# Token sums of the feed-forward weights begun while the output projection still runs

## The chip, the cores and the metric

One core of a Trainium2 chip runs one program. The time is the device time of one execution in microseconds; a kernel's time is the median of several executions. Its engines are TensorE (PE, matmuls, with weight loads as PEld), VectorE (DVE), ScalarE (ACT), GpSimd (POOL) and SyncE (SP). SP, ACT and POOL also issue DMA transfers, which 16 DMA engines carry out. Each engine works through its own list of instructions in order, and waits on semaphores for what others produce. The order of each list is made when the program is built, by a scheduler that simulates the program.

## The reference

Two layers on a sequence of 1024 tokens of width 1024, batch 1, in float32. Layer 0 mixes tokens by windowed attention, layer 1 by a gated linear recurrence in both directions; each has cross attention heads beside it. What matters here is the seam between a layer's mixer and its feed-forward part:

```
h = h + rmsnorm(concat(o, cross) @ w_out, g1)        # output projection
u = rmsnorm(h, g2)
gate, up = split(u @ w_in)                           # 1024 -> 2 x 2816
f = (gelu(depthwise_conv3(gate) + b) * up) @ w_out2  # 2816 -> 1024
h = h + rmsnorm(f, g3)
```

## The kernel before

Every float32 product is made of three products of operands split into a high and a low part (wh and wl for weights, uh and ul for tokens): high by high, high by low, low by high. ScalarE makes the high part by a cast, VectorE the low part by a subtraction.

The **output projection** (class WOut, method finish) works on row tiles of 128 tokens, eight of them, in two column halves of 512. The first half makes y0 for all eight rows (one tile of 128 x 8 x 512) and POOL multiplies it with the gain g1. The second half then goes row by row, n = 0 to 7: TensorE makes 12 x 3 matmuls from oh and ol (split from `or`, which SP loads); VectorE multiplies with g1 (y1); the row's mean square goes to POOL, which raises it to the power -1/2 (prs); VectorE adds y0 and y1, scaled by prs, to the old row x (L537, two instructions); the row is stored (h1d); norm_T normalizes it: the sum of squares on ScalarE, the power on POOL (nrs), the scaling on VectorE (nu, L124), eight 128 x 128 transposes on TensorE (pt, L132), and the split into uh and ul. For n = 4 to 7 the differences dw (POOL, then VectorE) and xd (VectorE) are made too.

The **first feed-forward stage** (function ffn) multiplies 1024 x 1024 tokens with 22 weight pieces f of 1024 x (2 x 128). It replaces eight block products by seven, with sums of weight blocks and sums of token blocks. Per f the weights are four tiles: st holds blocks as they are, sx and sy hold sums. sx is loaded twice with the same 256 KB block by SP (L638), then POOL issues a DMA that adds 512 KB from memory to it (L641). sy is loaded by SP (512 KB, L639), then POOL issues two DMAs: one adds half of sx to half of sy (L642), the next half of sy to the other half (L643); each waits for the one before. They are called the token sums' weights, or the sums. Products 1 and 2 use st and write the banks X and Y; product 5 (sx) and 3 (sy) write V; product 6 (sy, with u6h and u6l), 7 (sx, with u7h and u7l) and 4 (st, with u4h and u4l) write X. The functions load, weights, operand and prod make these.

The first two f, and products 1 and 2 of the third, are written out in first_units: while the projection's last rows are still on their way, TensorE already runs products 1 and 2 on the tokens that are done; products 5, 6, 3, 7 and 4 follow. From then on the f follow in a steady loop.

Memory sets when the sums can begin. The tiles sx and sy belong to the pool of the FFN (fp), two of each. They are placed where the projection's tiles were, so SP's loads into them and POOL's adds wait for whatever used that place last. The order of POOL's and SP's instructions is the scheduler's; `tc.high_priority` puts a part ahead in it, and `behind(...)` makes an instruction issue after another.

## Time and profile before

| | us |
|---|---|
| median of 3 runs | 2749.36 |
| lowest and highest | 2745.89, 2750.08 |
| profiled execution, its own time | 2745.05 |
| its span in the trace | 2743.3 |
| TensorE busy in it | 2665.1 (97%) |

The mean clock that TensorE was granted is 0.992 of full speed. Layer 0's projection, second half, is at about 530 to 600 us of the trace and its first feed-forward products start at about 596; in layer 1 they start at about 2088. Row tile n = 6 has its transposes at 595.27 and 2087.36, row tile n = 7 at 607.10 and 2099.19. TensorE's matmuls overlap: a matmul is listed with about 0.39 us, but with nothing to wait for the next one starts 0.227 us later. A number in brackets behind a row is the time the engine stood idle before it, with what ended that wait.

### The profile page before, as it was taken

What the parts mean: (1) busy time and instruction counts of PE and PEld (TensorE: products, weight loads), DVE (VectorE), ACT (ScalarE), POOL (GpSimd) and SP (SyncE); (2) the same over time, 40 slices, a digit from 0 to 9 for tenths busy, and PEclk for the clock granted to TensorE, in tenths of its full rate; (3) what the DMA queues carried; (4) which work ended last, traced back from release to release, by engine and by line L of the source; (5) the groups of instructions that cost most, each with busy time, mean ns of one, the idle gap of its engine ahead of it and who ended that gap; (6) DMA issues with size and microseconds to landing.
All of it is one profiled execution on the core that took longest, in us unless ns stands there. A gap on an engine that the chain in (4) does not pass through costs nothing.

```text
span 2743.3 us, 37508 instructions
## 1 busy us (share of the span) xinstructions
PE 2665.1 (97%) x13448; PEld 2225.2 (81%) x13448; DVE 1818.9 (66%) x3039; ACT 1398.6 (51%) x2558; POOL 489.5 (18%) x537
## 2 busy tenths in 40 slices
PE   8999999999999999999999999999998999999998
PEld 7888887787888888887888888888787888887887
DVE  6588777677565555477686777868567756556446
ACT  6367667544444445454454545545454544444443
POOL 1231120221111100031232231312122111110012
PEclk9999998999999999999999999999999999999999
DMA  7683213668777757673234541111467777774666
GB/s 281 207 177 83 66 45 101 195 184 201 201 195 196 198 148 242 197 261 126 73 135 110 118 93 55 43 58 34 142 211 189 189 201 203 199 197 151 228 192 230
DMA packets 217035, 435.79 MB, mean 159 GB/s; under 512 B 20752, under 2 KB 77456, under 8 KB 211216
## 3 DMA queue, kind: packets, MB, share of 16 engines
q1 hardware_dynamic: 188416, 334.55, 37.5%
q0 software_dynamic: 25408, 92.29, 16.5%
q10 hardware_dynamic: 3024, 6.55, 0.6%
q8 instruction: 106, 1.74, 0.3%
q14 instruction: 81, 0.66, 0.1%
HBM read 338.42 MB, written 117.96 MB: 166 GB/s over the span
## 4 chain that ended last, share of the span: by engine, by line
PE 87%; DVE 6%; DMA 3%; ACT 2%; issue 2%; POOL 1%; SPq 0%; DVEq 0%; POOLq 0%; ACTq 0%
PE X L564 29%; PE V L564 10%; PE pj L84 8%; PE pj L85 7%; PE pj L86 7%; PE Y L564 4%; PE pb L84 3%; PE pb L85 3%; PE pb L86 3%; PE po L1192 1%; PE pa L1144 1%; PE pt L361 1%; PE pa L1124 1%; PE pu L1168 1%; DMA sx<-in_ffw_dram 1%
## 5 line engine op out<-in xcount | busy, mean ns | idle before, releaser
L89 DVE TENSOR_TENSOR wl<-st,wh 128x1024 fp32r<-128x1024 f32 (+1 forms) x242 | 262.9, 1090 | 351.7 <-ACT wh L89 332.0
L89 ACT CAST wh<-st 128x1024 fp32r<-128x1024 f32 (+1 forms) x242 | 225.6, 934 | 293.0 <-PE X L564 190.4
L84 PE MATMUL pj<-uh,wh 128*128 128x512 f32 x512 | 206.4, 403 | 6.4 <-DVE xl L89 4.6
L564 PE MATMUL X<-wl,wh 128*128 128x512 f32 x528 | 204.9, 390 | 0.3 <-DVE wl L89 0.3
L564 PE MATMUL X<-wh,wl 128*128 128x512 f32 x528 | 204.9, 390 | 0.0
L85 PE MATMUL pj<-ul,wh 128*128 128x512 f32 x512 | 203.2, 397 | 0.0
L86 PE MATMUL pj<-uh,wl 128*128 128x512 f32 x512 | 203.0, 396 | 0.0
L564 PE MATMUL X<-wh 128*128 128x512 f32 x528 | 199.8, 390 | 1.4 <-DVE c L920 1.4
L84 PE MATMUL pj<-wh,uh 128*128 128x384 f32 (+1 forms) x512 | 190.8, 373 | 0.4 <-DVE v L303 0.4
L85 PE MATMUL pj<-wl,uh 128*128 128x384 f32 (+1 forms) x512 | 186.9, 365 | 0.0
L86 PE MATMUL pj<-wh,ul 128*128 128x384 f32 (+1 forms) x512 | 186.7, 365 | 0.0
L564 PE MATMUL V<-uh,wl 128*128 128x512 f32 x352 | 137.2, 390 | 1.1 <-DVE wl L89 1.1
L564 PE MATMUL V<-uh,wh 128*128 128x512 f32 x352 | 137.8, 391 | 0.0
L564 PE MATMUL V<-ul,wh 128*128 128x512 f32 x352 | 137.7, 391 | 0.0
L80 DVE TENSOR_TENSOR wl<-st,wh 128x1024 fp32r<-128x1024 f32 (+1 forms) x86 | 107.4, 1255 | 26.2 <-ACT wh L79 25.3
L79 ACT CAST wh<-st 128x1024 fp32r<-128x1024 f32 (+1 forms) x96 | 96.7, 1014 | 51.1 <-PE pj L85 31.6
L1138 POOL TENSOR_TENSOR E<-EP,q 128x256 f32<-128x256 f32 x64 | 53.2, 831 | 371.0 <-DVE EP L1131 270.6
L84 PEld LDWEIGHTS pj<-uh,wh 128*128 128x128 f32 x512 | 97.2, 190 | 26.8 <-DVE xl L89 5.5
L564 PEld LDWEIGHTS X<-wh 128*128 128x128 f32 x528 | 99.1, 188 | 22.5 <-issue 1.8
L564 PEld LDWEIGHTS X<-wl,wh 128*128 128x128 f32 x528 | 99.1, 188 | 21.3 <-DVE wl L89 0.7
L564 PEld LDWEIGHTS X<-wh,wl 128*128 128x128 f32 x528 | 99.1, 188 | 20.7
L86 PEld LDWEIGHTS pj<-uh,wl 128*128 128x128 f32 x512 | 97.2, 190 | 19.6
(324 smaller groups left out, 7335.4 us busy)
## 6 DMA issues: line engine op xcount, KB each, us to landing
st<-hid SPq DMA_DIRECT2D x154, 256.0 KB, 3.2
st<-in_ffw_dram SPq DMA_DIRECT2D x110, 256.0 KB, 3.2
w2s<-in_ffw_dram POOLq DMA_DIRECT2D x24, 1024.0 KB, 7.8
st<-in_ffw_dram SPq DMA_DIRECT2D x44, 512.0 KB, 3.7
sx<-in_ffw_dram SPq DMA_DIRECT2D x88, 256.0 KB, 4.1
sy<-in_ffw_dram SPq DMA_DIRECT2D x44, 512.0 KB, 5.6
sx<-in_ffw_dram POOLq DMA_DIRECT2D x44, 512.0 KB, 8.3
hid<-tt SPq DMA_DIRECT2D x88, 256.0 KB, 4.4
```

Of the source, the lines that this page charges most:

```text
L79: act.copy(h[:, :n], raw)
L80: (eng or dve).tensor_tensor(l[:, :n], raw, h[:, :n].bitcast(F32), op=ALU.subtract)
L84: pe.matmul(o, ah, bh, start=first, stop=False)
L85: pe.matmul(o, ah, bl, start=False, stop=False)
L86: pe.matmul(o, al, bh, start=False, stop=last)
L89: return act.copy(h, src), dve.tensor_tensor(l, src, h.bitcast(F32), op=ALU.subtract)
L361: pe.transpose(tp[:, j, :], sm[:, j, c * P:(c + 1) * P], ident)
L564: pe.matmul(o, x, y, start=new, stop=e, skip_group_check=not first)
L1124: pe.matmul(pa[:, c, :], E2[:, cs], E1[:, cs], start=True, stop=True)
L1138: pool.tensor_tensor(gl, pl_, ql, op=ALU.mult)
L1144: pe.matmul(pa[eo:eo + n, c, lo:lo + n], G[:, c * P + eo:c * P + eo + n], G[:, c * P + lo:c * P + lo + n], start=True, stop=True, tile_pos ...
L1168: r["marks"][1:] = [pe.matmul(pu[:, c, :], kT[:, c, :], r["v"][:, 4 * b + c, :], start=True, stop=True)]
```

## The change

y0 is no longer one tile of the projection's pool but four tiles of two rows each, with the tags sx, sx, sy, sy, in a new pool `ys` that lives until the first feed-forward stage has ended. The FFN's sx and sy come from that pool too. So the place of y0's rows 0 and 1 becomes the first sx, that of rows 2 and 3 the second sx, that of rows 4 and 5 the first sy, that of rows 6 and 7 the second sy, each as soon as its two rows have been added to x.

The sums of f = 0 and 1 are written into the loop of the projection's second half: behind row n = 1 the two loads of the first sx, behind n = 2 its add, behind n = 3 and 4 the same for the second sx, behind n = 5 the load of the first sy, behind n = 6 its two adds, behind n = 7 the load of the second sy. The two adds of the second sy are in first_units. The loads of f = 2 and 3 are no longer issued behind a mark, and the conv constants (cw, cb, ncw) have a pool of their own, allocated later. The second feed-forward stage and the steady loop keep their code.

```diff
+    def sums_x(l, f, pl):
+
+        sx = pl.tile([P, 1024], F32, tag="sx", bufs=2, name="sx")
+        for c in range(2):
+            nc.sync.dma_start(sx[:, c * 512:(c + 1) * 512], A["ffw1"][l, f, :, :512])
+        return sx
+
+    def add_x(l, f, sx):
+        pool.dma_start(sx, A["ffw1"][l, f, :, 512:1536], accum_op=ALU.add, max_dma_last_dim=8192)
+
+    def sums_y(l, f, pl):
+        sy = pl.tile([P, 1024], F32, tag="sy", bufs=2, name="sy")
+        nc.sync.dma_start(sy, A["ffw1"][l, f, :, 1024:])
+        return sy
+
+    def add_y(sx, sy):
+        pool.dma_start(sy[:, :512], sx[:, :512], accum_op=ALU.add, max_dma_last_dim=8192)
+        pool.dma_start(sy[:, 512:], sy[:, :512], accum_op=ALU.add, max_dma_last_dim=8192)
...
+            self.yq = tc.alloc_tile_pool(name=f"ys{l}", bufs=1, side="right", reuse_waits="tile")
+            y2 = [self.yq.tile([P, 2, 512], F32, tag=t, bufs=2, name="y0") for t in ("sx", "sx", "sy", "sy")]
+            y0 = {t: y2[n // 2][:, n % 2, :] for n, t in enumerate(self.order)}
...
-            y0 = wp.tile([P, NT, 512], F32, bufs=1, name="y0")
...
+                if n in (1, 3):
+                    self.sx.append(sums_x(l, n // 2, self.yq))
+                elif n in (2, 4):
+                    add_x(l, n // 4, self.sx[-1])
+                elif n in (5, 7):
+                    self.sy.append(sums_y(l, n // 6, self.yq))
+                elif n == 6:
+                    add_y(self.sx[0], self.sy[0])
...
-        def load(f, a1=None, a22=None):
+        def load(f, a1=None):
...
-            if a22 is None:
-                a22 = raw()[:, :512]
-            sx, sy = [fp.tile([P, 1024], F32, tag=t, bufs=2, name=t) for t in ("sx", "sy")]
-            for c in range(2):
-                nc.sync.dma_start(sx[:, c * 512:(c + 1) * 512], w[:, :512])
-            last_load[0] = nc.sync.dma_start(sy, w[:, 1024:])
+            a22 = raw()[:, :512]
+            sx, sy = sums_x(l, f, wo.yq), sums_y(l, f, wo.yq)
             nc.sync.dma_start(a22, w[:, 512:1024])
-            pool.dma_start(sx, w[:, 512:1536], accum_op=ALU.add, max_dma_last_dim=8192)
-            pool.dma_start(sy[:, :512], sx[:, :512], accum_op=ALU.add, max_dma_last_dim=8192)
-            pool.dma_start(sy[:, 512:], sy[:, :512], accum_op=ALU.add, max_dma_last_dim=8192)
+            add_x(l, f, sx)
+            add_y(sx, sy)
...
-                raws = {f: load(f, a1[f], a22[:, f * 512:(f + 1) * 512]) for f in range(2)}
+                r = raw()
+                a22 = [r[:, f * 512:(f + 1) * 512] for f in range(2)]
+                for f in range(2):
+                    nc.sync.dma_start(a22[f], A["ffw1"][l, f, :, 512:1024])
+                raws = {f: (a1[f], wo.sx[f], wo.sy[f], a22[f]) for f in range(2)}
                 a1.append(raw(A["ffw1"][l, 2, :, 1024:]))
+                add_y(wo.sx[1], wo.sy[1])
...
-            with behind(last_load):
-                raws[2] = load(2, a1[2])
-                raws[3] = load(3)
+            raws[2] = load(2, a1[2])
+            raws[3] = load(3)
```

The scheduler then orders the engines anew. POOL, layer 0, from the nrs of row n = 5 to the end of the projection, before (sx_6595 and sy_6596 are f = 0, sx_6604 and sy_6605 f = 1; dw_6439 and dw_6535 belong to rows 6 and 7):

```order
L102 TENSOR_TENSOR nrs_6340<-nms_6338,nhalf_76 128x1
L128 TENSOR_TENSOR dw_6439<-uh_78,ul_79 128x512
L102 TENSOR_TENSOR prs_6426<-pms_6424,nhalf_76 128x1
L102 TENSOR_TENSOR nrs_6436<-nms_6434,nhalf_76 128x1
L128 TENSOR_TENSOR dw_6535<-uh_78,ul_79 128x512
L102 TENSOR_TENSOR prs_6522<-pms_6520,nhalf_76 128x1
L102 TENSOR_TENSOR nrs_6532<-nms_6530,nhalf_76 128x1
L641 DMA sx_6595<-in_ffw1_dram 128x1024
L641 DMA sx_6604<-in_ffw1_dram 128x1024
L642 DMA sy_6596<-sx_6595 128x512
L642 DMA sy_6605<-sx_6604 128x512
```

The same stretch now (sx_5991 and sy_6375 are f = 0, sx_6179 and sy_6571 f = 1):

```order
L102 TENSOR_TENSOR nrs_6354<-nms_6352,nhalf_76 128x1
L410 DMA sy_6375<-sx_5991 128x512
L128 TENSOR_TENSOR dw_6455<-uh_78,ul_79 128x512
L411 DMA sy_6375<-sy_6375 128x512
L102 TENSOR_TENSOR prs_6442<-pms_6440,nhalf_76 128x1
L102 TENSOR_TENSOR nrs_6452<-nms_6450,nhalf_76 128x1
L128 TENSOR_TENSOR dw_6553<-uh_78,ul_79 128x512
L102 TENSOR_TENSOR prs_6540<-pms_6538,nhalf_76 128x1
L410 DMA sy_6571<-sx_6179 128x512
L102 TENSOR_TENSOR nrs_6550<-nms_6548,nhalf_76 128x1
L411 DMA sy_6571<-sy_6571 128x512
```

Both adds of f = 0's sy now stand ahead of row 6's prs, and the first add of f = 1's sy ahead of row 7's nrs; the two adds of sx stand further ahead, behind the nrs of rows 1 and 3. In layer 1 the first two come directly one behind the other, ahead of dw.

VectorE, layer 0, from the last nu on, before:

```order
L124 SCALAR_TENSOR_TENSOR nu_6528<-x_6512,nrs_6532,g2_5755 128x1024
L89 TENSOR_TENSOR wl_6633<-st_6613,wh_6632 128x1024
L135 TENSOR_TENSOR dw_6535<-dw_6535,pt_6537 128x512
L89 TENSOR_TENSOR ul_79<-pt_6545,uh_78 128x4x128
L140 TENSOR_TENSOR xd_5487<-pt_6545,dw_6535 128x4x128
L89 TENSOR_TENSOR ul_79<-dw_6535,uh_78 128x4x128
L720 TENSOR_TENSOR u_6620<-Y_6618,s1_6660 128x512
L720 TENSOR_TENSOR u_6621<-Y_6619,s1_6687 128x512
L579 TENSOR_SCALAR ncw_6569<-cw_6565 128x66
L89 TENSOR_TENSOR wl_6718<-sx_6595,wh_6717 128x1024
L89 TENSOR_TENSOR wl_6722<-sx_6604,wh_6721 128x1024
L591 SCALAR_TENSOR_TENSOR u6l_6586<-xd_5487,u6h_6585 128x1024 x2
```

And now:

```order
L124 SCALAR_TENSOR_TENSOR nu_6546<-x_6530,nrs_6550,g2_5761 128x1024
L89 TENSOR_TENSOR wl_6640<-st_6618,wh_6639 128x1024
L89 TENSOR_TENSOR wl_6725<-sx_5991,wh_6724 128x1024
L89 TENSOR_TENSOR wl_6729<-sx_6179,wh_6728 128x1024
L748 TENSOR_TENSOR u_6628<-Y_6626,s1_6694 128x512
L135 TENSOR_TENSOR dw_6553<-dw_6553,pt_6555 128x512
L89 TENSOR_TENSOR wl_6737<-sy_6375,wh_6736 128x1024
L89 TENSOR_TENSOR ul_79<-pt_6563,uh_78 128x4x128
L140 TENSOR_TENSOR xd_5487<-pt_6563,dw_6553 128x4x128
L89 TENSOR_TENSOR ul_79<-dw_6553,uh_78 128x4x128
L622 SCALAR_TENSOR_TENSOR u6l_6598<-xd_5487,u6h_6597 128x1024 x2
L89 TENSOR_TENSOR wl_6741<-sy_6571,wh_6740 128x1024
```

The low parts of both sx and of the first sy now stand ahead of row 7's last ul, the one of `ul<-dw`, which product 5 needs; the first u stands ahead of nu, and ncw further behind.

More of the change, by code (lines that the diff above doesn't have):

```diff
@@ L510, in finish @@
                 if t in self.part:
-                    dve.tensor_tensor(y0[:, t, :], ps, self.part[t], op=ALU.add)
+                    dve.tensor_tensor(y0[t], ps, self.part[t], op=ALU.add)
                 else:
-                    act.copy(y0[:, t, :], ps)
-                sumsq(wp, y0[:, t, :], s0[:, t:t + 1])
+                    act.copy(y0[t], ps)
+                sumsq(wp, y0[t], s0[:, t:t + 1])
             with tc.issue_after(after.ins):
@@ L522, in finish @@
             for t in self.order:
-                pool.tensor_tensor(y0[:, t, :], y0[:, t, :], g1[:, :512], op=ALU.mult)
+                pool.tensor_tensor(y0[t], y0[t], g1[:, :512], op=ALU.mult)
             for n, t in enumerate(self.order):
@@ L535, in finish @@
                 rs = rstd_of(wp, ss, 1, D, "p")
-                for c, y in ((slice(0, 512), y0[:, t, :]), (slice(512, 1024), y1)):
+                for c, y in ((slice(0, 512), y0[t]), (slice(512, 1024), y1)):
                     dve.scalar_tensor_tensor(x[:, c], y, rs[:, 0:1], x[:, c], op0=ALU.mult, op1=ALU.add)
@@ L587, in ffn @@
             B[k] = tuple(u2p.tile([P, 4, 512], F32R, name=f"u{k}{c}") for c in "hl")
+        cp = tc.alloc_tile_pool(name=f"cw{l}", bufs=1, reuse_waits="tile")
+        cw = cp.tile([P, NF, 3], F32, name="cw")
+        cb = cp.tile([P, NF], F32, name="cb")
+        nc.sync.dma_start(cw, A["conv_w"][l])
+        nc.sync.dma_start(cb, A["conv_b"][l])
+        ncw = cp.tile([P, NF, 3], F32, name="ncw")
+        dve.tensor_scalar_mul(ncw, cw, -1.0)
         def nsplit(h, l_, src):
```

14 lines of the change are left out of this document (4 added, 10 removed).

## The prediction

> **What bounds the kernel now.** I read four views in this order: the page's busy times, the windows around the start of each feed-forward stage, TensorE's timeline there, and the chain of waits behind its longest stop. The page comes first:
>
> ```profile
> PE 2665.1 (97%) x13448; PEld 2225.2 (81%) x13448; DVE 1818.9 (66%) x3039; ACT 1398.6 (51%) x2558; POOL 489.5 (18%) x537
> ```
>
> TensorE is busy 2665.1 of 2743.3 us, so an edit that leaves its matmuls alone can win 78 us at most. The windows show how much of that lies where the change works (columns: window, length, then busy us of PE, PEld, DVE, ACT, POOL with counts, granted clock, DMA share, GB/s):
>
> ```profile
> 607.00:627.00 20.00, 14.18 (x61) 10.60 (x60) 9.91 (x12) 8.79 (x13) 4.31 (x5) 0.96 0.93 208
> 627.00:647.00 20.00, 19.30 (x80) 15.19 (x80) 18.34 (x19) 9.69 (x13) 4.35 (x5) 0.96 0.82 189
> 2095.00:2115.00 20.00, 16.97 (x76) 12.88 (x74) 10.17 (x13) 7.22 (x11) 5.53 (x7) 1.00 0.91 197
> 2115.00:2135.00 20.00, 18.97 (x74) 14.71 (x74) 16.91 (x17) 8.52 (x12) 4.36 (x6) 0.91 0.89 191
> ```
>
> Layer 0 loses 5.82 + 0.70 us here, layer 1 loses 3.03 + 1.03 us and a bit after 2135. TensorE's timeline names each stop in brackets:
>
> ```profile
> 595.27 1.06 PE L132 MATMUL pt<-ident,nu 128*128 128x128 f32 x8 [0.53 <-DVE nu L124]
> 607.10 1.04 PE L132 MATMUL pt<-ident,nu 128*128 128x128 f32 x8
> 610.49 0.39 PE L564 MATMUL X<-uh,wl 128*128 128x512 f32 x1
> 611.34 0.50 PE L564 MATMUL Y<-uh,wh 128*128 128x512 f32 x1 [0.47 <-DVE u L720]
> 615.57 0.50 PE L564 MATMUL V<-uh,wl 128*128 128x512 f32 x1 [0.53 <-DVE wl L89]
> 625.69 0.80 PE L564 MATMUL X<-u6h,wh 128*128 128x512 f32 x1 [4.83 <-ACT wh L89]
> 628.75 0.39 PE L564 MATMUL X<-u6h,wl 128*128 128x512 f32 x1
> 628.98 0.40 PE L564 MATMUL X<-u6h,wh 128*128 128x512 f32 x1
> 645.17 0.50 PE L564 MATMUL X<-u6h,wh 128*128 128x512 f32 x1 [0.69 <-ACT wh L89]
> 2087.36 1.06 PE L132 MATMUL pt<-ident,nu 128*128 128x128 f32 x8 [3.15 <-DVE nu L124]
> 2116.03 0.50 PE L564 MATMUL X<-u6h,wh 128*128 128x512 f32 x1 [3.09 <-ACT wh L89]
> 2135.83 0.50 PE L564 MATMUL X<-u6h,wh 128*128 128x512 f32 x1 [0.69 <-ACT wh L89]
> ```
>
> The long stop is for the split weight wh. The chain of waits says what made it late (start, length, what; the last row is layer 1's, the others layer 0's):
>
> ```profile
> 600.92 2.58 DMA h1d<-x
> 604.12 11.10 DMA sx<-in_ffw_dram
> 615.51 0.86 POOL sy L642
> 618.17 6.35 DMA sy<-sy
> 2108.61 6.26 DMA sy<-sy
> ```
>
> So the sums are three accumulating transfers in series, and the first waits for a row store of the projection (600.92 + 2.58), because the memory of sx and sy in the FFN's pool lies where the projection's tiles were. From 604.12 to 618.17 + 6.35 that is 20.4 us of transfers one behind the other, and TensorE had run out of other products at 620.9.
>
> **The change part by part.** *Removed.* The sums of f = 0 and 1 are begun during row tiles 1 to 7, so the three stops that end in wh, wl or u fall away. Matmuls start 0.227 us apart (628.75, 628.98). From 610.49 to 611.34 is 0.85, that is 0.62 over, against 0.47 shown as idle: a stop costs 0.15 more than its bracket, and the matmul behind it is about 0.1 slow (0.50 for 0.39). Layer 0: 0.47 + 0.53 + 4.83 + 0.69 = 6.52, plus 4 x 0.25 = 1.0. The eight starts from 625.69 to 628.75 take 3.06 for 7 x 0.227 = 1.59: 1.47 lost at a lower clock.
>
> ```profile
> 625.00:635.00 10.00, 9.31 (x34) 7.53 (x35) 8.18 (x9) 5.12 (x7) 1.74 (x2) 0.83 0.94 225
> 2115.00:2125.00 10.00, 8.97 (x32) 6.92 (x33) 7.59 (x8) 4.79 (x7) 1.78 (x3) 0.83 0.99 220
> ```
>
> Layer 0 thus gives 9.0. In layer 1 the windows' idle 3.03 + 1.03 and the 0.69 at 2135.83 make 4.75, with 1.0 for four stops and 1.5 for the same clock row of 0.83: 7.3. Ceiling of the removal: 16.3 us. [...]
>
> *Moved onto POOL.* Each layer's six accumulating issues (0.86 us each, row of 615.51) leave the queue behind nrs of row 7 and enter between the rows' prs and nrs, the one-column powers that every row's normalization waits for. POOL works in order, so what waits there holds prs. These are the rows they slide between:
>
> ```profile
> 583.66 2.26 POOL L128 TENSOR_TENSOR dw<-uh,ul 128x512 f32<-128x512 f32 x1 [0.28 <-DVE ul L89]
> 587.81 0.55 POOL L102 TENSOR_TENSOR prs<-pms,nhalf 128x1 f32<-128x1 f32 x1 [1.88 <-DVE pms L100]
> 602.78 0.55 POOL L102 TENSOR_TENSOR nrs<-nms,nhalf 128x1 f32<-128x1 f32 x1 [4.31 <-DVE nms L100]
> 2075.10 1.67 POOL L128 TENSOR_TENSOR dw<-uh,ul 128x512 f32<-128x512 f32 x1 [2.77 <-DVE ul L89]
> 2078.05 1.40 POOL L102 TENSOR_TENSOR prs<-pms,nhalf 128x1 f32<-128x1 f32 x1 [1.28 <-DVE pms L100]
> 2093.57 0.55 POOL L102 TENSOR_TENSOR nrs<-nms,nhalf 128x1 f32<-128x1 f32 x1 [4.11 <-DVE nms L100]
> 580.62 0.33 SPq L538 DMA_DIRECT2D h1d<-x  x1
> 598.97 0.66 DVE x L537
> 603.36 1.28 DVE L124 SCALAR_TENSOR_TENSOR nu<-x,nrs,g 128x1024 f32<-128x1024 f32 x1 [0.73 <-POOL nrs L102]
> DMA to landing us min/median/max: 3.3/5.6/9.5
> DMA to landing us min/median/max: 3.3/5.3/7.8
> 565.00:575.00 10.00, 10.00 (x50) 8.37 (x49) 7.54 (x13) 4.70 (x10) 1.26 (x3) 1.00 0.42 145
> 585.00:595.00 10.00, 9.74 (x48) 7.81 (x46) 9.24 (x14) 6.38 (x11) 2.03 (x3) 1.00 0.64 209
> ```
>
> The two landing rows are those of the sy load and of the add sy<-sy, the last two are windows; the add sy<-sx was seen to free the next one 2.65 us after its start (615.51 to 618.17). The sums of sx I cost at nothing: POOL stands idle for 2 to 4 us before each power (the brackets), TensorE is without a gap up to 585 (10.00 of 10), and a hold longer than that would come back as a stop before pt of row 2 or 4.
> Row 6, layer 0: the sy load can start when row 5's first half is added, just ahead of the store at 580.62, say 580.0. It lands at 583.3 to 585.6 (minimum, median); the add is issued and dw (2.26) runs behind it to 586.4 to 588.7; the second add, 2.65 behind the first, ends at 587.3 to 589.5. prs is wanted at 587.81: a delay of 0 to 1.7, I take 0.5 since the DMA share there is 0.42 to 0.64 and not the 0.9 of the FFN's start. DVE has no room in that row (9.24 of 10 us), so it lands on the 0.53 stop at 595.27.
> Row 6, layer 1: the load starts at about 2069.5, lands at 2072.8 to 2075.1, the adds and dw (1.67) end at 2078.0 to 2081.5, against prs at 2078.05 that itself took 1.40: -0.6 to 3.0 (below nothing, because nu of that row now stands one ul, 0.6 us, earlier on DVE); I take 0.8, on top of the 3.15 stop at 2087.36.
> Row 7: the second sy load starts at 599.7, behind the first half of x (598.97 + 0.66); the add that waits for it on POOL stands ahead of nrs. It lands at 603.0 to 605.3, plus 0.86: nrs at 603.9 to 606.2 for 602.78, a delay of 1.1 to 3.4, I take 2. Behind nrs wait nu on DVE (1.28), and behind that wl of f = 2, both wl of sx, u, dw, wl of sy and ul, xd, ul: from 605.4 about 1.2 + 3 x 1.22 + 1.22 + 5 x 0.61 = 9.1 us, to 614.5. The transposes at 607.10 still find nu (606.6). TensorE, with no stop ahead, begins V 24 matmuls behind them: 607.9 + 5.4 = 613.3, its second matmul needs that last ul: a stop of 1.0 (0 to 2.4). In layer 1 the transposes come later behind nrs (2099.2 against 2093.57: 5.6, for 4.3), so 0.2 (0 to 1.1).
>
> *DVE.* It does the same work, in another order. In 607 to 627 it was busy 9.91 of 20 because the sums were late; now its wl come first and u6l, tt, u7l follow without gaps. Behind ul at 614.5: u6l 2.35, wl 1.22, four tt 4.7, ncw 0.2, then u7l, tt, u7l 3.6 and a u or two: 627 to 628, wanted at 613.3 + 72 x 0.227 = 629.7. The cover is 2 to 3 us; I charge 0.5 per layer for what slips.
>
> *Moved transfers.* Two sx, two sy and six adds per layer leave a stretch with a DMA share of 0.93 and enter one of 0.42 to 0.64. The row loads of the projection share SP's queue and these engines; with that room I charge nothing; if they slipped a microsecond per row, TensorE would lose up to 8 us a layer, since then each row would start late. The other edits (conv constants and ncw loaded later, y0 in four tiles of the same total size, the loads of f = 2 and 3 no longer held behind the earlier ones) are under the same covers and cost nothing.
>
> *Sum.* -9.0 + 0.5 + 1.0 + 0.5 = -7.0 in layer 0; -7.3 + 0.8 + 0.2 + 0.5 = -5.8 in layer 1; together -12.8 (from -16.9 with row 6 of layer 1 gaining, to -7 with every hold at its upper end). The profiled execution took 2745.05 us (span 2743.3), which becomes 2732; it lies 4.3 under the median of the runs shown, 2749.36, so that median becomes 2736.5.
>
> **The rivals.**
> *Half of it.* The POOL holds come at the medians and not near the minima: row 6 +1.7 and +3.0, row 7 +2.4 and +1.1, 1.0 for DVE: 9.2 off 16.3 leaves 7, that is 2742. For it: the medians are of all 44 loads. Against: those ran in stretches with fuller queues.
> *DVE becomes the bound.* 18.34 of 20 us busy in 627 to 647 speaks for it. If u7l misses its 629.7 by 2 us in each layer, on top of my holds, 9 us remain: 2740. Against: 11.8 us of its idle time from 607 to 647 are set free.
> *The issue itself starves.* POOL and DVE do hinder each other here; the next rows are a nu that ran beside dw, and the group of the sx adds' issues.
>
> ```profile
> 2084.93 2.29 DVE nu L124
> L641 POOL DMA_DIRECT2D sx<-in_ffw_dram x44: 868/871/1225, 603.5 to 2466.8; - x44
> ```
>
> For it: that nu took 2.29 for 1.28, and prs at 2078.05 took 1.40 for 0.55. If an accumulating issue waited out a DVE instruction of that length, each would take 0.86 + 2.3 = 3.2 us. Two ahead of row 6 and one ahead of row 7 add 4.6 + 2.3 a layer, 13.8 in all, and next to nothing is left: 2749. Against: in 627 to 647, with DVE at 18.34 of 20, issues ran, and all 44 took 0.87 in the median and 1.23 at most.
> [...]
> *The other side.* POOL stands in its queue for the landing before row 6. At the longest landings, 9.5 for the load and 7.8 for the add, prs of row 6 comes at 580 + 9.5 + 0.86 + 7.8 + 0.86 = 599.0, 11.2 late, 12 in layer 1 with dw. Each such stop also slows the clock (1.5): 26 lost against 16.3 won, 2759. A queue of one landing alone does not reach that. It decides from 8 us of hold per layer. Against: rows of 0.42 to 0.64 DMA share.
>
> **How the numbers follow.** Forecast 0.57, half 0.16, DVE 0.09, starved issue 0.06, other side 0.07, the sums moved without being what is late 0.05 (no change). A measurement of this kernel tells about 0.2%, 5.5 us, from no change: faster means below 2743.9. Forecast and DVE fall there nearly always (0.64), half of it in two of three (0.11), one in a hundred of the rest: 0.76; same 0.16; slower 0.08. The range goes from 2728 (every hold at its minimum, median as the profiled run) to 2747, past the half case and into no change; for the forecast alone it is 2731 to 2741.
>
> **What would show it.** In the profile after: no PE stop for wh near the third group of products, DMA share below 0.9 there, the granted clock 1.00; the stop before pt of row 6 longer by up to 2 us; nrs of row 7 at its sy issue's end; a stop of about 1 us for ul before V in layer 0. I am wrong if pt of rows 2 to 6 waits many us for nu, if or loads hold the projection, or if the wh stop moves to the sums of f = 2.

## The result and the profile after

The changed kernel took 2730.68 us (median of 6 runs, 2726.46 to 2733.57) against 2748.27 us before (6 runs): a ratio of 0.9935, 95% interval 0.9922 to 0.9948. That is 17.6 us less, inside the range, and just below the 2731 to 2741 that the forecast gave for its own mechanism. The profiled execution fell by 18.6 us, from 2743.3 to 2724.7 of span. (Two executions among the experiments below took 5358 and 4425 us, one of the kernel with the begun sums alone and one of the repeated kernel with moves by 256; the times given for these two kernels are without them.) The reason given for the gain was only partly right, and the first line of the page after says so:

```profile
PE 2648.1 (97%) x13448; PEld 2224.4 (82%) x13448; DVE 1818.9 (67%) x3039; ACT 1398.3 (51%) x2558; POOL 485.8 (18%) x537
```

TensorE's busy time fell from 2665.1 to 2648.1 us with the same 13,448 matmuls. Its idle time, which the forecast meant to shorten first of all, went from 78.2 to 76.6 us.

The start of each feed-forward stage, in the windows of the kernel after (columns as in the prediction):

```profile
595.00:615.00 20.00, 16.60 (x72) 14.04 (x73) 16.11 (x25) 9.32 (x15) 4.70 (x6) 0.83 0.51 142
615.00:635.00 20.00, 20.00 (x90) 16.57 (x89) 19.01 (x21) 9.64 (x13) 4.38 (x6) 1.00 0.82 191
2080.00:2100.00 20.00, 18.43 (x84) 15.66 (x85) 16.33 (x23) 7.48 (x13) 4.30 (x6) 0.89 0.48 132
2100.00:2120.00 20.00, 20.00 (x90) 16.57 (x89) 19.35 (x21) 10.30 (x13) 5.23 (x6) 1.00 0.76 170
```

From 615 and from 2100 on TensorE does not stop at all: every stop for wh, wl and u that the prediction had listed is gone. Ahead of that, one stop in each layer is much longer. TensorE's timeline of the kernel after, the transposes of row 6 in both layers:

```profile
598.40 1.94 PE L132 MATMUL pt<-ident,nu 128*128 128x128 f32 x8 [6.17 <-DVE nu L124]
2081.57 1.94 PE L132 MATMUL pt<-ident,nu 128*128 128x128 f32 x8 [6.43 <-DVE nu L124]
```

They were 0.53 and 3.15 before, and the eight transposes now take 1.94 us for 1.06, at half the clock (0.50 granted from 598.40 to 600.34, 0.83 as the mean of the window from 595). The chain of waits of the kernel after shows what made them late (start, length, what):

```profile
579.32 5.60 DMA sy<-in_ffw_dram
585.47 0.89 POOL sy L410
586.36 1.31 POOL dw L128
590.03 0.87 POOL sy L411
590.90 0.60 POOL prs L102
591.52 1.41 DVE x L559 x2
598.40 1.94 PE pt L132 x8
```

POOL stands for the landing of sy, then for the landing of its first add, and only then does row 6's prs. VectorE's timeline shows the price as seen from the row: it had asked at 585.73 and went on at 591.52.

```profile
585.73 0.15 DVE L100 TENSOR_SCALAR pms<-ss 128x1 f32<-128x1 f32 x1
591.52 1.41 DVE L559 SCALAR_TENSOR_TENSOR x<-y,prs,x 128x512 f32<-128x512 f32 x2 [5.64 <-POOL prs L102]
```

So the removed stops and the new ones nearly cancel, and the time came from somewhere else. TensorE runs its matmuls in almost the same order in all these kernels (316 of 13,448 stand elsewhere in the change), so matmul number N of one trace can be set against number N of another. The difference in start time from the kernel before, and what each stretch adds to it (us; numbers 2960, 3550, 5000, 10480, 11000 and 12600 are the bounds, worked out from the start times of the traces; the two right columns are the first two experiments):

```
                            change   consts behind               sums alone
ahead of layer 0's seam      -2.5          -1.9                       +0.2
layer 0: row 6 to the loop   -3.0          -2.6                       -2.5
layer 0: steady loop         -4.7          -4.7                        0.0
up to layer 1's seam         +1.2          +0.9                       +1.6
layer 1: row 6 to the loop   -4.2          +1.8                       -2.5
layer 1: steady loop         -5.3          -5.3                        0.0
at the last matmul          -18.6         -11.4                       -3.2
```

Ten of the 18.6 us come from the two steady loops, where neither kernel has a stop. The windows of these loops show it in the number of their matmuls. First the kernel before; its row from 1090 is the second feed-forward stage, whose matmuls are of the same size:

```profile
700.00:1000.00 300.00, 300.00 (x1306) 245.06 (x1305) 173.26 (x188) 132.43 (x170) 38.96 (x45) 1.00 0.75 197
1090.00:1190.00 100.00, 100.00 (x443) 82.81 (x442) 49.80 (x47) 49.97 (x65) 13.14 (x8) 1.00 0.60 190
2160.00:2460.00 300.00, 300.00 (x1305) 245.01 (x1304) 175.32 (x190) 135.20 (x174) 39.83 (x46) 1.00 0.77 200
```

Then the kernel after:

```profile
700.00:1000.00 300.00, 300.00 (x1326) 248.39 (x1325) 174.09 (x187) 135.73 (x173) 38.94 (x45) 1.00 0.75 194
2160.00:2460.00 300.00, 300.00 (x1325) 248.43 (x1324) 174.31 (x188) 135.74 (x174) 40.69 (x47) 1.00 0.78 202
```

TensorE is called busy all 300 us in both, at full clock, with 1306 matmuls in one and 1326 in the other (the ones that only reach into the window are counted too). The same tile f to f, in TensorE's timeline of the kernel before and of the kernel after:

```profile
747.04 0.40 PE L564 MATMUL X<-u4h,wh 128*128 128x512 f32 x1
766.37 0.40 PE L564 MATMUL X<-u4h,wh 128*128 128x512 f32 x1
```

```profile
741.14 0.39 PE L594 MATMUL X<-u4h,wh 128*128 128x512 f32 x1
760.18 0.39 PE L594 MATMUL X<-u4h,wh 128*128 128x512 f32 x1
```

A period of 84 matmuls takes 19.33 us before and 19.04 after, that is 0.2301 and 0.2267 us from one start to the next. Taken apart, the step before was 0.234 us in the 36 that read u4, u6 or u7, and 0.227 in the 48 that read uh and ul; after it is 0.227 in all. What differs for these tiles is their address. The small conv tiles (cw, cb, ncw) used to lie ahead of them in the FFN's pool. In the built program u4, u6 and u7 began at byte 171328 of a partition and on, which leaves the rest 64 modulo 256, while wh, wl, uh and ul leave 160; with the conv tiles behind them they begin at 154272 and on, which leaves 160 too. That part of the change was described as a pool of its own for the conv constants and costed at nothing. (u4, u6 and u7 are the sums of token blocks; the text ahead used "token sums" for the weight sums sx and sy that are multiplied with them.)

### The profile page after: what moved, and what is told of

It reads as the page before. It is cut to its first block, busy times and chain, and to the rows that moved or that the text cites. A ratio compares the mean times of both kernels' runs of the same rounds, so it can differ in the third digit from the quotient of the medians.

```text
span 2724.7 us, 37495 instructions
## 1 busy us (share of the span) xinstructions
PE 2648.1 (97%) x13448; PEld 2224.4 (82%) x13448; DVE 1818.9 (67%) x3039; ACT 1398.3 (51%) x2558; POOL 485.8 (18%) x537
## 4 chain that ended last, share of the span: by engine, by line
PE 86%; DVE 7%; DMA 2%; ACT 2%; issue 2%; POOL 1%; SPq 0%; DVEq 0%; POOLq 0%; ACTq 0%
PE X L594 29%; PE V L594 11%; PE pj L84 8%; PE pj L85 7%; PE pj L86 7%; PE Y L594 4%; PE pb L84 3%; PE pb L85 3%; PE pb L86 3%; PE po L1221 1%; PE pa L1173 1%; PE pt L361 1%; DMA or<-oT 1%; PE pa L1153 1%; PE pu L1197 1%
## 5 line engine op out<-in xcount | busy, mean ns | idle before, releaser
L89 DVE TENSOR_TENSOR wl<-st,wh 128x1024 fp32r<-128x1024 f32 (+1 forms) x242 | 262.9, 1090 | 341.0 <-ACT wh L89 329.6
```

Source lines behind the costliest of these rows:

```text
L89: return act.copy(h, src), dve.tensor_tensor(l, src, h.bitcast(F32), op=ALU.subtract)
```

## The experiments

**The address alone.** The kernel before with the conv tiles behind u4, u6, u7. The order of every engine's instructions is unchanged.

```diff
-        cw = fp.tile([P, NF, 3], F32, name="cw")
-        cb = fp.tile([P, NF], F32, name="cb")
...
             B[k] = tuple(u2p.tile([P, 4, 512], F32R, name=f"u{k}{c}") for c in "hl")
+        cp = tc.alloc_tile_pool(name=f"cw{l}", bufs=1, reuse_waits="tile")
+        cw = cp.tile([P, NF, 3], F32, name="cw")
+        cb = cp.tile([P, NF], F32, name="cb")
...
```

> The kernel before with one edit: the three small conv tiles (cw, cb, ncw; 616 bytes in a partition, 672 with the rounding) are allocated behind u4, u6, u7 and not ahead of them. The order of every engine's instructions is that of before; only addresses move: u4, u6, u7 go from rest 64 modulo 256 to rest 160, the rest of the weight tiles wh and wl. Theory 'address': the changed kernel's steady feed-forward loop takes 19.04 us per f for 19.33 before, without any stop in either, so the 36 of 84 matmuls that read u4, u6, u7 started 0.008 us late each. 22 f in two layers make 44 x 0.29 = 12.8 us: about 2735.5, ratio 0.9953, period 19.04, and the stops for wh, wl and u at the start of each feed-forward stage unchanged. Rival 'sums': the loop runs faster because its sums come earlier: here nothing changes, 19.33 and ratio 1.000.

Measured: 2737.14 us, ratio 0.9963 (0.9950 to 0.9975). The period is 19.04 us in both layers, and the loops give the same -4.7 and -5.3 as the change (table above). Its windows:

```profile
700.00:1000.00 300.00, 300.00 (x1325) 248.49 (x1324) 174.06 (x187) 136.04 (x174) 39.01 (x45) 1.00 0.75 196
2160.00:2460.00 300.00, 300.00 (x1325) 248.49 (x1324) 177.10 (x192) 134.82 (x173) 41.62 (x48) 1.00 0.79 204
```

Theory "address" holds for the loops. The whole gain is 11.0 us by the medians (7 to 14 by the interval), a little below the 12.8 expected. In the profiled execution the stops for wh stayed, as they should, but not with their lengths: in layer 0 they were 1.67 and 1.98 us for 4.83 and 0.69, in layer 1 they were 0.51 and 5.21 for 3.09 and 0.69. The longest of them:

```profile
2128.01 0.80 PE L564 MATMUL X<-u6h,wh 128*128 128x512 f32 x1 [5.21 <-ACT wh L89]
```

**The begun sums alone.** The changed kernel with the conv tiles ahead of u4, u6, u7 again.

```diff
+        cp = tc.alloc_tile_pool(name=f"cw{l}", bufs=1, reuse_waits="tile")
+        cw = cp.tile([P, NF, 3], F32, name="cw")
+        cb = cp.tile([P, NF], F32, name="cb")
+        ncw = cp.tile([P, NF, 3], F32, name="ncw")
         fp = tc.alloc_tile_pool(name=f"ff{l}", bufs=1, reuse_waits="tile")
...
```

> The changed kernel with the small conv tiles put ahead of u4, u6, u7 again, so that these have their old rest (64 modulo 256) while the sums are begun in the projection as in the change. Theory 'address': the period stays at 19.33, the 12.8 us are not won, what is left is the begun sums' own gain: 18.6 between the two profiles, less 12.8, less about 1 that already differs ahead of layer 0's projection and in the second mixer, that is 4 to 5 us: about 2743.5, ratio 0.9982. Rival 'sums': 2730.5, ratio 0.9935.

Measured: 2743.64 us (median of nine), ratio 0.9990 (0.9981 to 1.0000). The period is 19.33 again (1306 matmuls in 300 us), the loops give 0.0, and the two seams give -2.5 each. So what the forecast was about, the sums begun in the projection, is worth about 5 us in this profile and 3 us by the ratio of the runs, not 12.8; the interval of the ratio goes from 5 us to no change.

**Which rest, and against what.** Pads ahead of u4, u6, u7 in the changed kernel, all orders unchanged:

```diff
         for k in (4, 6, 7):
+            u2p.tile([P, ((8, 8, 8), (32, 8, 8))[l][(4, 6, 7).index(k)]], F32, name=f"pad{k}")
             B[k] = tuple(u2p.tile([P, 4, 512], F32R, name=f"u{k}{c}") for c in "hl")
```

> The changed kernel with pads of 32 to 128 bytes ahead of u4, u6 and u7; every engine's order is that of the change. Rests modulo 256 against that of the weights (160): in layer 0 u4 +32, u6 +64, u7 +96; in layer 1 u4 +128, u6 +160, u7 +192. Theory 'modulo 64': the matmuls of u4 in layer 0 and of u6 in layer 1 and u7 in layer 0 (odd multiples of 32) start 0.231 to 0.238 apart, the others 0.227; per layer 19.04 plus 0.097 for each slow product: 19.23 in layer 0 and 19.14 in layer 1. Theory 'modulo 128': only u4 of layer 1 stays at 0.227: 19.33 and 19.23. Theory 'modulo 256': all six are slow: 19.33 in both.

Measured: 2743.53 us in one execution; 19.32 us per f in both layers. Moves by 32, 64, 96, 128, 160 and 192 bytes all cost (the matmuls of the six moved tile pairs are 0.230 to 0.235 us apart in the mean; 64 bytes cost least): "modulo 64" and "modulo 128" fall, "modulo 256" stands. Then the other operand: the weights moved by 32 bytes, the tokens where they were.

```diff
+    padp = tc.alloc_tile_pool(name="padr", bufs=1)
+    padp.tile([P, 8], F32, name="padr")
     ring = tc.alloc_tile_pool(name="ring", bufs=RING)
     up = tc.alloc_tile_pool(name="uT", bufs=1)
+    up.tile([P, 56], F32, name="padu")
...
```

> The changed kernel with wh and wl of the ring moved by 32 bytes (rest 192 modulo 256) while uh, ul, u4, u6 and u7 keep theirs (160); every engine's order is that of the change. Theory 'difference': it is the difference between the two operands' rests that costs, so now all 84 matmuls of an f start about 0.235 apart: 19.04 + 84 x 0.0081 = 19.7 us per f, 44 x 0.68 = 30 us in the two loops and more in the projections, 2765 or above. Theory 'token address': what costs is the rest of the token tiles alone (64 modulo 256, or not 32 modulo 64): nothing changes, 19.04 and 2730.

Measured: 2765.2 us in one execution. The windows of this kernel, the last one in the second feed-forward stage:

```profile
700.00:1000.00 300.00, 300.00 (x1288) 241.54 (x1287) 173.27 (x188) 131.10 (x168) 39.56 (x46) 1.00 0.75 195
2160.00:2460.00 300.00, 300.00 (x1287) 241.55 (x1286) 173.88 (x187) 134.98 (x173) 39.90 (x46) 1.00 0.76 197
1090.00:1190.00 100.00, 100.00 (x443) 82.84 (x442) 47.66 (x42) 48.42 (x61) 7.96 (x5) 1.00 0.61 192
```

19.60 us per f, now with a step of 0.233 in all 84 matmuls, uh and ul among them, whose addresses keep their rest. The second stage takes both operands from the ring, both now with the rest 192, and has its 443 matmuls as before. So the step goes with the difference of the two operands' rests and not with the token tiles' address alone: uh and ul kept theirs and went from 0.227 to 0.233. And 160 is no better a rest than 192: with both operands on either, the second stage has 443 matmuls in these 100 us. Last, moves by whole multiples of 256:

```diff
         for k in (4, 6, 7):
+            if k < 7:
+                u2p.tile([P, ((64, 64), (56, 8))[l][(4, 6).index(k)]], F32, name=f"pad{k}")
             B[k] = tuple(u2p.tile([P, 4, 512], F32R, name=f"u{k}{c}") for c in "hl")
```

> The changed kernel with pads: in layer 0 u4 is moved by 256 bytes, u6 and u7 by 512; in layer 1 u4 by 224, u6 and u7 by 256. Every engine's order is that of the change. The run with pads of 32 to 192 bytes had 19.32 us per f in both layers, 0.28 over the change. Theory 'modulo 256': layer 0 stays at 19.04, and layer 1 pays for u4 alone, a third of it: 19.13. Theory 'modulo 512': in layer 0 u4 pays (19.13), in layer 1 all three (19.32). Theory 'any move costs' (the exact distance of the change is special): 19.32 in both.

That execution took 12799 us, with matmuls about 1.3 us apart in every stage of its first two thirds, the kernel before at 2748.64 beside it; nothing on addresses can be read from it, and the kernel was run again.

> The same kernel as the run before, whose execution took 12799 us because TensorE ran its matmuls 1.32 us apart from the first to the last third and 0.82 after, in every stage alike, which says nothing on addresses. Theory 'modulo 256': 19.04 us per f in layer 0, 19.13 in layer 1. Theory 'modulo 512': 19.13 and 19.32. Theory 'any move costs': 19.32 in both.

Measured: 2734.47 us (median of three). The windows of this run:

```profile
700.00:1000.00 300.00, 300.00 (x1325) 248.43 (x1324) 175.07 (x190) 135.75 (x174) 38.94 (x45) 1.00 0.76 197
2160.00:2460.00 300.00, 300.00 (x1318) 247.14 (x1317) 177.11 (x191) 134.55 (x173) 41.50 (x48) 1.00 0.77 200
```

19.04 us in layer 0, where the tiles are 256 and 512 bytes away, and 19.15 in layer 1, where u4 is off by 224 and u6 and u7 by 256. In TensorE's timeline of this run the tiles moved by 256 and 512 keep their step (layer 0: 0.226 for u4, u6 and u7; layer 1: 0.227 for u7), and u4 of layer 1, moved by 224, does not (0.234). There u6, moved by 256, runs behind u4, and its first five steps are slow too (0.231, the next six 0.227). Of the three theories "modulo 256" alone agrees with the two periods.

**The POOL hold.** The four adds of the first two sy behind nrs of row 7:

```diff
-                elif n == 6:
-                    add_y(self.sx[0], self.sy[0])
...
-                add_y(wo.sx[1], wo.sy[1])
+                with behind(powered):
+                    for f in range(2):
+                        add_y(wo.sx[f], wo.sy[f])
...
```

> The changed kernel with the four adds of both first sy (two of f = 0 in row 6, two of f = 1) put behind nrs of row 7 on POOL; the loads, the adds of sx and all addresses stay. Theory 'POOL hold': prs of row 6 stood in POOL's queue behind the add that waits for the sy load and the one that waits for the first add (prs was wanted at 585.8 and ran at 590.6), which made the stops of 6.17 and 6.43 before the transposes of row 6 and the half clock behind them. Without them the stops go back to 0.5 and about 3, the clock stays whole in layer 0: 5.6 + 3.3 less stop and 2 to 4 us of clock, 10 to 13 us, and the sums still come in time (the last add lands at about 613, its product is at 619): 2718 to 2721, ratio 0.989 to 0.990. Rival 'row 6 is late for other reasons' (DVE without room, the loads beside it): stops of 6 stay, ratio 0.9935. Rival 'the wait moves': a stop for wh of the first sy comes back, 3 us or more in each layer, ratio 0.991 or above.

Measured: 2729.62 us, ratio 0.9939 (0.9917 to 0.9960): no faster than the change. TensorE's timeline of this kernel shows two things at once:

```profile
595.98 1.87 PE L134 MATMUL pt<-ident,nu 128*128 128x128 f32 x8 [3.62 <-DVE nu L126]
616.29 0.73 PE L594 MATMUL V<-uh,wh 128*128 128x512 f32 x2 [0.36 <-ACT uh L89]
617.64 0.50 PE L594 MATMUL V<-ul,wh 128*128 128x512 f32 x1 [0.61 <-DVE ul L89]
2080.88 1.94 PE L134 MATMUL pt<-ident,nu 128*128 128x128 f32 x8 [2.70 <-DVE nu L126]
2102.51 0.73 PE L594 MATMUL V<-uh,wh 128*128 128x512 f32 x2 [1.71 <-ACT uh L89]
```

The stops before row 6's transposes fell, by 2.55 and 3.73 us: the hold was there. But it was not the whole stop in layer 0, and the gain went into a new one before V. In the lists of ScalarE and VectorE the split of the first sy stands ahead of row 7's last uh and ul; with the adds later that split waits for sy, and uh and ul wait behind it.

**Other places.** The rows' places handed out as sx, sy, sx, sy, so that f = 0 is complete by row 4:

```diff
-            y2 = [self.yq.tile([P, 2, 512], F32, tag=t, bufs=2, name="y0") for t in ("sx", "sx", "sy", "sy")]
+            y2 = [self.yq.tile([P, 2, 512], F32, tag=t, bufs=2, name="y0") for t in ("sx", "sy", "sx", "sy")]
...
```

> The changed kernel with the places of y0's rows given in the order sx, sy, sx, sy: f = 0's sums are complete by row 4 (load of sx behind row 1, add behind row 2, load of sy behind row 3, its two adds behind row 4), f = 1's sx is loaded behind row 5 and added behind row 6, its sy loaded behind row 7. Ahead of row 6's prs POOL now has one add that waits for a load of two times 256 KB instead of two adds in series. Theory 'POOL hold': the hold shrinks from about 5 us to 0 to 3, the hold at row 4 fits into the slack of that row: stops before the transposes of row 6 of 0.5 to 3 in layer 0 and 3 to 5 in layer 1, 2718 to 2726, ratio 0.989 to 0.992. Rival 'any add ahead of prs holds as long': 0.9935. Rival 'row 4 has no slack': a new stop before its transposes, ratio 0.995 or above.

Measured: 2733.27 us, ratio 0.9947 (0.9932 to 0.9962), the change's own time within the intervals. TensorE's timeline of this kernel:

```profile
584.03 1.94 PE L132 MATMUL pt<-ident,nu 128*128 128x128 f32 x8 [2.88 <-DVE nu L124]
2085.06 1.94 PE L132 MATMUL pt<-ident,nu 128*128 128x128 f32 x8 [5.66 <-DVE nu L124]
```

The first row is that of row 4's transposes in layer 0, the second that of row 6's in layer 1. The hold moved to row 4; in layer 0 it came out as a stop there, with another of 2.35 left before row 6, and layer 1 kept its long stop before row 6 although only an sx add stands ahead of that row's prs. The slack that earlier rows have on POOL's brackets did not cover the hold. VectorE makes up a part only of what it has lost: in the change, layer 0, its y of row 2 came 1.5 us later against TensorE than in the kernel before, and that of row 6 was still 0.7 late.

**The list order mended.** Late adds, and the splits of sy issued behind row 7's split of dw, the first u behind row 7's nu:

```diff
...
+                last_diff[0] = split(*d, w)
...
+                    with behind(wo.mark[1:]):
                         dve.tensor_tensor(u[f][:, ti], y, s1, op=ALU.add)
...
+            with behind(last_diff[0]):
                 nx(0)
                 nx(1)
...
```

> The kernel with the late sy adds (four adds behind nrs of row 7) and two edits of order: the splits of both first sy issue behind row 7's split of dw on VectorE and ScalarE, and the first u issues behind row 7's nu. In the late-adds run the stops before row 6's transposes fell from 6.17 and 6.43 to 3.62 and 2.70, but new ones stood before V: 0.36 + 0.61 + 0.79 in layer 0 and 1.71 + 0.61 in layer 1, since wl of sy stood ahead of row 7's last ul. Theory 'POOL hold, gain eaten by the list order': those stops go, with their slower matmuls 2.5 and 4.5 us, the stops of row 6 stay at about 3.6 and 2.7: 6 to 7 us below the change in the same call, ratio to before 0.991. Rival 'the sums are late there': a stop for wh of sy takes their place, no difference from the change.

Measured: 2722.95 us, ratio 0.9904 (0.9888 to 0.9919), with the change itself at 2733.26 beside it (0.9942, below): 10.3 us less. The stops before V are gone; in TensorE's timeline the long ones left are

```profile
600.33 1.94 PE L134 MATMUL pt<-ident,nu 128*128 128x128 f32 x8 [3.62 <-DVE nu L126]
2079.95 1.06 PE L134 MATMUL pt<-ident,nu 128*128 128x128 f32 x8 [3.55 <-DVE nu L126]
```

So the gain of the run with late adds had indeed been eaten by the order of the lists. The seams give -5.5 and -8.4 us here against before, and the addresses have about 2.6 of that.

**VectorE beside POOL.** In the change, VectorE's timeline has one small subtraction of row 2 that took five times its usual 0.42:

```profile
548.13 2.12 DVE L89 TENSOR_TENSOR ol<-or,oh 128x256 fp32r<-128x256 f32 x1 [0.23 <-ACT oh L89]
```

It ran beside POOL's dw (listed from 548.35, 1.61 us long), which the first sx add had pushed there. (In the kernel before, dw also costs VectorE something at this row, 1.52 us for a pair of subtractions of which a like pair takes 1.02 at 545.23 in the run with ul first, so that row 2 came 1.5 us later than before, not 1.7.) How the two engines hinder each other is not shown, nor which of the two came second: dw is listed 0.2 us behind the subtraction, and starts on POOL are rough. The kernel with ul first, with the sx adds issued behind that dw:

```diff
-                elif n in (2, 4):
-                    add_x(l, n // 4, self.sx[-1])
+                elif n == 4:
+                    with behind(dws[-1:]):
+                        for f in range(2):
+                            add_x(l, f, self.sx[f])
...
```

> As the run with ul first, and the adds of sx issue behind the dw of row 4 on POOL. In the change, the first sx add goes ahead of that dw, and dw then runs beside a small subtraction of row 2 on VectorE (ol of 256 columns), which took 2.12 us for 0.42; from there on every later row's y on VectorE is 1.3 us late in layer 0 against TensorE. Theory 'VectorE beside dw': with the old place of dw that subtraction takes 0.4 again, rows 2 to 6 come 1.5 earlier, the stops of row 6 shrink by about 1.5 in each layer: 3 us below the run with ul first. Rival 'VectorE catches up before row 6': no difference.

Measured: 2720.92 us, ratio 0.9896 (0.9881 to 0.9911); against the run with ul first the intervals overlap. In layer 1 the theory shows in the trace: y of rows 2 to 6 on VectorE, which had come 0.7 to 1.9 us late against TensorE in the run with ul first, is on its old time to 0.2 us, and the stop fell from 3.55 to 1.86. In layer 0 it did not, since row 5 lost 2.7 us for another reason. TensorE's timeline of this kernel:

```profile
601.13 1.07 PE L134 MATMUL pt<-ident,nu 128*128 128x128 f32 x8 [3.61 <-DVE nu L126]
2080.59 1.06 PE L134 MATMUL pt<-ident,nu 128*128 128x128 f32 x8 [1.86 <-DVE nu L126]
```

The change as it is, measured beside these two:

> The changed kernel as it is, on the same chip as the two others, so that they can be set against it: 0.9935 of before again, stops of about 6 us before row 6's transposes in both layers, 19.04 us per f.

Measured: 2733.26 us, ratio 0.9942 (0.9929 to 0.9955), within the first measurement's interval. Its stops before row 6's transposes were longer still in this execution, 8.55 and 8.75 us in its timeline:

```profile
605.81 1.94 PE L132 MATMUL pt<-ident,nu 128*128 128x128 f32 x8 [8.55 <-DVE nu L124]
2092.28 1.94 PE L132 MATMUL pt<-ident,nu 128*128 128x128 f32 x8 [8.75 <-DVE nu L124]
```

and its seams gave -0.2 and -1.6 us against before, where the first profile of the change had -3.0 and -4.2. The loops gave -4.7 and -5.3 in both. So the loops repeat to 0.1 us, while the seams of one kernel differ by 5 us from one execution to the next: the 5 us that the begun sums alone gave in one profile are no more certain than that.

**The row loads beside the adds.** What made row 5 late in layer 0 is seen in the transfers from 560 to 580 us: the two loads of `or` with 256 KB for the projection, kernel before, then kernel after (KB each, median us to landing).

```profile
or<-oT SPq DMA_DIRECT2D x2, 256.0 KB, 3.4
```

```profile
or<-oT SPq DMA_DIRECT2D x2, 256.0 KB, 5.7
```

The second sx add, 512 KB, is in flight beside the first of them, which took 7.2 us for 3.8; the other took 4.1 for 3.1. The kernel with dw first, with that add moved behind row 5's nrs:

```diff
                     with behind(dws[-1:]):
-                        for f in range(2):
-                            add_x(l, f, self.sx[f])
+                        add_x(l, 0, self.sx[0])
...
+                    if n == 5:
+                        with behind(powered):
+                            add_x(l, 1, self.sx[1])
...
```

> As the run with dw first, and the second sx add issues behind row 5's nrs on POOL and not behind row 3's. In every run with the sums begun early, the row load of 567 to 576 us that is in flight beside that 512 KB add landed 7.1 to 7.3 us after its issue, in the kernel before 3.4 in the median; ScalarE and VectorE then start row 5 and 6 about 3 us later against TensorE, and a stop of 3.6 us before row 6's transposes is left in layer 0. Theory 'DMA engines shared': with the add gone from there the load lands in 4 us, the stop falls from 3.61 to 1 or less in layer 0 and by 0 to 1 in layer 1: about 3 us below the run with dw first, ratio to before 0.988 to 0.9885. Rival 'the stop is VectorE's own work in row 6': it stays at 3.6, no difference.

Measured: 2722.67 us, ratio 0.9900 (0.9883 to 0.9917), no difference from the run before it. The stop in layer 0 stays; rows of TensorE, ScalarE and VectorE of this kernel:

```profile
600.04 1.94 PE L134 MATMUL pt<-ident,nu 128*128 128x128 f32 x8 [3.63 <-DVE nu L126]
561.28 0.62 ACT L89 CAST oh<-or 128x512 fp32r<-128x512 f32 x1 [2.44 <-DMA or<-oT]
587.39 3.24 DVE L126 SCALAR_TENSOR_TENSOR nu<-x,nrs,g 128x1024 f32<-128x1024 f32 x1 [0.45 <-POOL nrs L104]
```

The `or` loads from 560 to 580 land in 4.0 us, as expected, and row 5 loses nothing more. But in this execution the row load at 561 was late beside the first add (2.44), and row 5's nu, now beside the moved add and dw on POOL, took 3.24 us for 1.27. So the 3.6 us of layer 0 has at least two sources that take each other's place, a row load beside an add and VectorE beside POOL; the runs do not settle how much of it would be left without either. A third lies ahead of the sums: in the runs with late adds, ul first, dw first, this one and the change again, layer 0's y of row 0 on VectorE came 1.8 to 2.7 us later against TensorE than in the kernel before (0.0 in the first profile of the change), before any load of the sums had been issued. No run shows why, nor how much of it reaches row 6. In layer 1, without lateness of any row, 1.86 us are left of the stop (3.15 in the kernel before).

## Why the prediction was right, and where its steps were wrong

- *The stops for wh, wl and u* (-9.0 and -7.3): right in kind. None of the eight is in the trace after.
- *Row 6 on POOL* (0.5 and 0.8 charged, bounds to 1.7 and 3.0): this is the term that was mis-sized. The mechanism was the one described, but sy took 5.6 us, its median and not its minimum of 3.3, and the second add came 4.6 us behind the first (585.47 to 590.03) and not 2.65. Row 6 went on 4.9 us late (585.73 to 591.52, less the 0.9 that pms and prs take when nothing holds them). The 2.65 was read from two rows that do not belong together. POOL's timeline of the kernel before, and the landings of its adds sy<-sx:

```profile
611.81 0.86 POOL L642 DMA_DIRECT2D sy<-sx  x1 [6.47 <-DMA sx<-in_ffw_dram]
615.51 0.86 POOL L642 DMA_DIRECT2D sy<-sx  x1 [2.84 <-DMA sx<-in_ffw_dram]
618.17 0.86 POOL L643 DMA_DIRECT2D sy<-sy  x1 [1.80 <-DMA sy<-sx]
DMA to landing us min/median/max: 3.3/3.9/7.6
```

By the order of POOL's instructions the first row is f = 0's, the second f = 1's, the third f = 0's again: the add at 618.17 waited for the one issued at 611.81, 6.4 us earlier, and none of the 44 landed in less than 3.3. With 4.6 in place of 2.65, and the 0.5 us between the landing of sy and the first add, the upper bound of 1.7 becomes about 3.7. The rest came from row 5, which was late itself: row 6 asked for prs 6.7 us after the start of sy's load, where the prediction had 7.8. The stops grew by 5.6 and 3.3 us in the first profile and by 8.0 and 5.6 in the other, beyond the bounds, and behind each the clock was at half (1.94 us for eight transposes that take 1.06).
- *Row loads "charged nothing"*: wrong. The one beside the second sx add landed in 7.2 us for 3.8, in a stretch whose DMA share had been 0.42 before.
- *The sums of sx "costed at nothing"*: wrong. Row 2 came 1.5 us later on VectorE, beside dw, and 0.7 of it was left at row 6. The slack was read off POOL's brackets; the engine with too little slack was VectorE.
- *Row 7, V and VectorE's own bound* (2.2 together): nothing of it was seen; TensorE, stopped before row 6, came later than assumed. The stops before V in the run with late adds (1.0 us in layer 0 and 2.3 in layer 1) are no proof of these terms, since there row 7's ul waited behind the split of a sy that had been made late. No run tests them alone.
- *"The other edits cost nothing"*: wrong, and by the largest amount. The place of the conv tiles was worth 10.0 us in the two loops, and by the period (0.287 for each of 44 f) 12.6 in all, the other 2.6 at the seams. The profile of before had it in plain view: 0.2301 us per matmul in the first stage's loop and 0.2267 in the second stage's, same shape, full clock, no stop. The two rows that the prediction quotes for 0.227 (628.75 and 628.98) read u6 and are 0.23 apart. The prediction read stops, and time lost inside "busy" has none.

Together: the begun sums gave 3 us by the runs (0 to 5) where 12.8 were forecast, less than the rival "half of it" (7); the addresses gave 11 by the runs and 12.6 by the period where none were forecast. The two errors cancel to within 5 us: that the number came out right was luck. The removed stops themselves, with their ceiling of 16.3, were not far off: with the adds late and the lists mended the seams, less the addresses' 2.6, give 11.4 us (ul first) and 14.0 (dw first) in their profiles.

The rival "the issue itself starves" fell: the issues of the begun sums on POOL took 0.86 to 0.97 us. What the rows show instead is VectorE slower beside POOL's dw, at two places: the subtraction with 2.12 us for 0.42 in the change, and a nu with 3.24 for 1.27 in the run with the second sx add later, there beside the issue of that add too, which itself took 0.90.

The fastest kernels are those with ul first, 0.9904, with dw first, 0.9896, and with the second sx add later, 0.9900 of before, which their intervals do not tell apart; the first two beat the change (0.9942) that was measured beside them.

## What to carry to other kernels

Divide a loop's busy time by its matmuls and set that against another stage with the same shape: a TensorE that is busy without a gap can still be slow (1.5% over this loop, 3% in the matmuls concerned), and neither the busy share nor the list of waits will say so. A wait put into an in-order queue is paid by whatever stands behind it (here row 6's prs, 4.9 us late), so price it by the engine with the least slack in that stretch and by the landings of that very transfer, not by the idle brackets of the queue itself or by the distance of two rows that may belong to different tiles. When a removed stop brings nothing, look for the next instruction in the lists that was ordered around the old one: here two edits of order turned no gain over the change into 10 us.

## What the runs showed of the hardware

- Matmuls of 128 x 512 began 0.227 us apart where the moving tile's address and the weights' leave the same rest modulo 256 (both 160 in the change; both 192 in the second stage of the run with the weights moved, with 443 matmuls in 100 us as before). Where they do not, the mean of a token tile was 0.230 to 0.235: with pads of 32, 64, 96, 128, 160 and 192 bytes, and 0.234 with 224. Moves by 256 and 512 left 0.226 to 0.227, but for the first five steps of layer 1's u6 behind the slow u4 (0.231). Moving the weights by 32 bytes instead of the tokens costs as well (0.233 in all). Why the two operands' addresses matter together was not tried.
- A stop of 3.62 us had half the clock behind it in one run (ul first, layer 0: 1.94 us for eight transposes at 600.33) and one of 3.61 had not in another (dw first, layer 0: 1.07 at 601.13). The clock was at half behind stops of 2.70 (late adds, layer 1: 1.94 at 2080.88) and 2.88 us too (other places, layer 0: 1.94 at 584.03), but not behind 3.15 (before, layer 1: 1.06 at 2087.36) and 3.55 (ul first, layer 1: 1.06 at 2079.95). So the length of the stop alone does not tell. In the change, layer 0, the granted clock was still 1.00 in the first 3.99 us of row 6's stop of 6.17, and 0.50 in the 6.83 us from 596.22 to 603.05, most of which lies behind the stop; in the kernel before it was 0.50 from 625.20 to 628.60, around the end of the stop of 4.83 for wh. How much idle time it takes was not measured, nor what sets the length of the slow stretch.
